# A convolution kernel's first loads: a smaller uncast head as one transfer, and the first pair's cast load moved behind the identity

## The chip, the core and the metric

The kernel runs on one core of one Trainium2 chip. The time is the device time of one execution in microseconds (us); smaller is better. Where a run was profiled, the "span" is the time from its first to its last instruction, about 1.8 us less than the measured time. All "landings" are the moments at which the trace shows the completion of a transfer on the last of the 16 DMA engines, if nothing else is said.

## The reference, cut to what matters

A 3 x 3 convolution with padding 1, in float32, of 16 images of 64 channels and 64 x 64 points, to 128 output channels:

```python
x      = randn(16, 64, 64, 64)                       # float32, 16.8 MB
weight = randn(128, 64, 3, 3) * (random(...) > 0.9)  # float32, 0.29 MB
output[b, co] += weight[co, ci, kh, kw] * x_pad[b, ci, kh:kh+64, kw:kw+64]
# output: (16, 128, 64, 64) float32, 33.6 MB
```

Every input byte has to be read and every output byte written: 50.6 MB.

## The kernel before

Two images make a "pair": 2 x 64 channels fill the 128 partitions. TensorE computes with bf16. Loads that convert float32 to bf16 on the way ("cast loads") are issued by GpSimd. Since the first products should not wait for them, the first 36 rows of pair 0, the "head", are loaded as float32 by the sync engine's queue, in two pieces, and cast by VectorE and ScalarE:

```python
HEAD = 36
nc.sync.dma_start(out=w_sb, in_=weight...)
x_head = const_pool.tile([128, HEAD, W], FP32, name="x_head")
for a, b in ((0, 9), (9, HEAD)):
    nc.sync.dma_start(out=x_head[:, a:b, :], in_=pair(0)[:, a:b, :])
nc.gpsimd.dma_start(out=xs[0][:, HEAD:H, :], in_=pair(0)[:, HEAD:H, :])
ident = const_pool.tile([128, 128], BF16, name="ident")
make_identity(nc, ident)                  # two short GpSimd instructions
for p in range(1, NP):
    nc.gpsimd.dma_start(out=xs[p], in_=pair(p))
# ... (27 idle matmuls to warm TensorE, casts and transposes of the weights)
cast_x(nc.vector.tensor_copy, 0, 9)
# ...
cast_x(nc.scalar.copy, 9, 18)
# ...
cast_x(nc.vector.tensor_copy, 18, HEAD)
```

Pair 0 begins with two "direct" products of 8 rows each (rows 0 to 15; they read rows 0 to 16). All other rows go in blocks of 16, for which GpSimd first adds neighbouring rows:

```python
def twos(p, o, r0):
    s = s_pool.tile([128, 8, W], BF16, name="s")
    nc.gpsimd.tensor_tensor(out=s, in0=xs[p][:, r0:r0+16:2, :],
                            in1=xs[p][:, r0+1:r0+16:2, :], op=ADD)
    # ... TensorE: 6 matmuls on s, 24 on xs[p]; VectorE adds and writes to o
for p in range(NP):
    # ... blocks of the pair, then
    if not last:
        for n in range(2):
            nc.sync.dma_start(out=out[2*p+n], in_=o[n])      # 2 MB each
    # the last pair in four pieces of 1 MB
```

## Time and profile before

| | before |
|---|---|
| time, median of the first 4 runs | 132.19 us (131.78 to 132.26) |
| span of the profiled run | 130.3 us |
| TensorE goes on with the second direct product at | 14.71 us |
| TensorE begins the first matmul on GpSimd's sums at | 18.50 us |
| end of the chain's TensorE part | 117.10 us |
| last store landed | 129.16 us |
| DMA queue empty (holes) | about 92 to 94.7 and 104 to 107.5 us |

### The profile page before, as it was taken

The page shows a single profiled execution, that of the slowest core. Times are in us where ns is not written, and L with a number is a line of the kernel's source. Part 1 is how long each engine was busy: PE and PEld are TensorE (multiplying, and loading weights), DVE is VectorE, ACT ScalarE, POOL GpSimd, SP SyncE. Part 2 cuts the span into 40 slices and gives each one's busy share as a digit, 9 for nine tenths or more (in the row PEclk, how much of TensorE's full clock was granted, in tenths as well). Part 3 has the DMA queues.
Part 4 walks back from the last instruction along what each step waited for, and adds up shares of the span by engine and source line. Part 5 has one row for each costly group of instructions (what it writes and reads, how often), then busy time and mean ns, then how long its engine had stood idle before and what let it go on. Part 6 is the DMA issues. An engine that isn't in the chain of part 4 may idle for free.

```text
span 130.3 us, 2488 instructions
## 1 busy us (share of the span) xinstructions
PE 110.6 (85%) x1002; PEld 56.0 (43%) x1002; DVE 83.0 (64%) x136; ACT 38.0 (29%) x70; POOL 40.7 (31%) x45
## 2 busy tenths in 40 slices
PE   6662499999999999999999999999999999993000
PEld 6430144445444544454445445544544454440000
DVE  0350425778777868787777777777777777777000
ACT  3500313333333333333243333333333333330000
POOL 6900463333333333333333333324333330000000
PEclk9985559999999999999999999999999999999655
DMA  4999999999999999999999999999599929999990
GB/s 136 217 297 228 216 209 226 209 216 216 302 325 307 327 322 314 362 428 438 423 425 428 433 423 433 428 428 443 244 408 403 403 86 402 458 385 415 415 410 18
DMA packets 4188, 42.99 MB, mean 330 GB/s; under 512 B 464, under 2 KB 464, under 8 KB 976
## 3 DMA queue, kind: packets, MB, share of 16 engines
q1 hardware_dynamic: 3024, 35.03, 64.6%
q0 software_dynamic: 1152, 7.80, 29.1%
q8 instruction: 8, 0.13, 0.4%
q14 instruction: 4, 0.03, 0.1%
HBM read 17.07 MB, written 33.55 MB: 389 GB/s over the span
## 4 chain that ended last, share of the span: by engine, by line
PE 79%; DMA 9%; DVE 1%; issue 1%; SPq 1%; ACT 1%; DVEq 0%
PE ps L136 79%; DMA x_head<-in_x_dram 9%; DVE o L169 1%; ACT x L88 1%; DVEq L215 0%; SPq L63 0%; SPq L60 0%; DVEq L169 0%
## 5 line engine op out<-in xcount | busy, mean ns | idle before, releaser
L136 PE MATMUL ps<-x,wT 64*128 64x504 bf16 (+3 forms) x780 | 91.4, 381 | 6.7 <-ACT x L88 4.2
L169 DVE TENSOR_TENSOR o<-ps,pc 128x512 f32<-128x512 f32 x124 | 77.8, 686 | 22.4 <-PE ps L136 20.1
L136 PEld LDWEIGHTS <-wT 64*128 64x128 bf16 x966 | 52.4, 96 | 60.4 <-issue 10.4
L155 POOL TENSOR_TENSOR s<-x 128x512 bf16<-128x512 bf16 x31 | 35.6, 1152 | 65.6 <-PE ps L136 43.4
L162 ACT COPY pc<-ps 128x512 f32<-128x512 f32 x62 | 33.3, 589 | 64.3 <-issue 61.8
L136 PE MATMUL ps<-s,wT 64*128 64x512 bf16 (+1 forms) x186 | 25.8, 380 | 0.0
L88 DVE CAST x<-x_head 128x576 bf16<-128x576 f32 (+1 forms) x2 | 1.2, 611 | 7.5 <-DMA x_head<-in_x_dram 7.5
L75 PE MATMUL ps<-idle_rhs 128*128 128x128 bf16 x27 | 3.1, 313 | 1.0 <-DVE idle_rhs L72 1.0
L68 POOL DMA_DIRECT2D x<-in_x_dram x7 | 3.7, 551 | 0.0
L150 DVE COPY o<-ps 128x512 f32<-128x512 f32 x2 | 1.4, 688 | 3.4 <-PE ps L136 3.4
L75 PEld LDWEIGHTS <-idle_rhs 128*128 128x128 bf16 x27 | 2.8, 149 | 1.0 <-DVE idle_rhs L72 1.0
L88 ACT CAST x<-x_head 128x576 bf16<-128x576 f32 x1 | 0.7, 672 | 8.2 <-DMA x_head<-in_x_dram 8.2
L92 DVE CAST w_bf<-w_sb 128x192 bf16<-128x192 f32 (+1 forms) x4 | 1.2, 360 | 2.5 <-DMA w_sb<-in_weight_dram 2.5
L149 ACT COPY o<-ps 128x512 f32<-128x512 f32 x2 | 1.2, 582 | 3.6 <-PE ps L136 3.6
L92 ACT ACT_TABLE_LOAD x1 | 1.3, 1283 | 0.7 <-PEq L204 0.7
L98 PE MATMUL ps<-ident,w_bf 128*128 128x128 bf16 x9 | 1.2, 308 | 0.0
L92 ACT CAST w_bf<-w_sb 128x64 bf16<-128x64 f32 (+1 forms) x2 | 0.7, 417 | 1.4 <-DMA w_sb<-in_weight_dram 1.4
L102 DVE TENSOR_TENSOR wT<-ps,wT 128x384 bf16<-128x384 f32 x2 | 1.0, 549 | 0.0
L98 PEld LDWEIGHTS <-w_bf 128*128 128x128 bf16 x9 | 0.8, 130 | 0.4 <-DVE w_bf L92 0.4
L64 POOL DMA_DIRECT2D x<-in_x_dram x1 | 0.7, 696 | 0.8 <-POOLq L204 0.8
L72 DVE MEMSET idle_rhs<- 128x64 uint32 x1 | 0.1, 112 | 0.8 <-PEq L204 0.8
L111 ACT CAST wT<-ps 128x384 bf16<-128x384 f32 x1 | 0.5, 478 | 0.4 <-PE ps L98 0.4
(8 smaller groups left out, 1.9 us busy)
## 6 DMA issues: line engine op xcount, KB each, us to landing
out_dram<-o SPq DMA_DIRECT2D x14, 2048.0 KB, 14.4
x<-in_x_dram POOLq DMA_DIRECT2D x7, 1024.0 KB, 26.1
out_dram<-o SPq DMA_DIRECT2D x4, 1024.0 KB, 9.4
x_head<-in_x_dram SPq DMA_DIRECT2D x1, 864.0 KB, 12.3
x<-in_x_dram POOLq DMA_DIRECT2D x1, 448.0 KB, 8.8
w_sb<-in_weight_dram SPq DMA_DIRECT2D x1, 288.0 KB, 2.7
x_head<-in_x_dram SPq DMA_DIRECT2D x1, 288.0 KB, 6.0
```

Of the source, the lines that this page charges most:

```text
L68: nc.gpsimd.dma_start(out=xs[p], in_=pair(p))
L75: nc.tensor.matmul(idle_ps, idle_rhs, idle_rhs, start=True, stop=True)
L88: copy(out=xs[0][:, a:b, :], in_=x_head[:, a:b, :])
L92: copy(out=w_bf4[:, g, a:b, :], in_=w_v[:, k : k + b - a, :])
L98: nc.tensor.matmul(wps[:, j, :], src, ident, start=True, stop=True)
L102: nc.vector.tensor_tensor(out=wT[:, g], in0=wps, in1=wT[:, G1], op=SUB)
L136: nc.tensor.matmul(ps[n][:, lo:hi, c_lo:c_hi], tap(g, kw, n), src[q, a:b:step, c_lo + kw - 1 : c_hi + kw - 1], start=(i == 0), stop=(i == ...
L149: nc.scalar.copy(out=o[0][:, r0 : r0 + rows, :], in_=ps[0])
L150: nc.vector.tensor_copy(out=o[1][:, r0 : r0 + rows, :], in_=ps[1])
L155: nc.gpsimd.tensor_tensor(out=s, in0=xs[p][:, r0 : r0 + 16 : 2, :], in1=xs[p][:, r0 + 1 : r0 + 16 : 2, :], op=ADD)
L162: nc.scalar.copy(out=c, in_=shared[n])
L169: nc.vector.tensor_tensor(out=o[n][:, first : r0 + 16 : 2, :], in0=ps[n], in1=pc[n], op=ADD)
```

## The change

The intent, in its author's words: "Only 18 rows of the first pair loaded uncast, as one transfer behind the weights; GpSimd issues the cast loads of all other rows straight away". The two direct products read 17 of these 18 rows.

```diff
-    HEAD = 36
+    HEAD = 18
...
-    for a, b in ((0, 9), (9, HEAD)):
-        nc.sync.dma_start(out=x_head[:, a:b, :], in_=pair(0)[:, a:b, :])
-    nc.gpsimd.dma_start(out=xs[0][:, HEAD:H, :], in_=pair(0)[:, HEAD:H, :])
+    nc.sync.dma_start(out=x_head, in_=pair(0)[:, 0:HEAD, :])
     ident = const_pool.tile([128, 128], BF16, name="ident")
     make_identity(nc, ident)
+    nc.gpsimd.dma_start(out=xs[0][:, HEAD:H, :], in_=pair(0)[:, HEAD:H, :])
...
-    cast_x(nc.scalar.copy, 9, 18)
+    cast_x(nc.scalar.copy, 9, HEAD)
     difference(G01, ps0)
     difference(G21, ps2)
-    cast_x(nc.vector.tensor_copy, 18, HEAD)
```

So there are three edits in one: fewer uncast rows (A), one transfer in place of two (B), and pair 0's cast load behind the identity in GpSimd's order (C). C makes GpSimd issue that load a little later, not sooner: at 1.43 us in place of 1.23 in the two traces.

## The prediction

> **What bounds the kernel now.** I read the page's digit rows first (slices of 3.26 us: PE is at 9 from the sixth slice on, DMA from the second), then the chain that ended last in order of time, then the timeline of the first 30 us, the DMA issues, and last the stages. The chain's middle:
>
> ```profile
> 1.65 12.31 DMA x_head<-in_x_dram
> 13.96 0.02 issue
> 13.98 0.68 ACT x L88
> 14.66 0.04 issue
> 14.71 102.39 PE ps L136 x936
> ```
>
> Columns: start, length, what. One transfer, the second piece of the uncast head (rows 9 to 35), holds the chain for 12.31 us; then TensorE runs without a gap until 117.10. So TensorE's start is what can be won, as long as nothing else bounds the end. Timeline (start, length, engine, line, what, count, idle before it and who ended it):
>
> ```profile
> 1.23 0.70 POOL L64 DMA_DIRECT2D x<-in_x_dram  x1 [0.79 <-POOLq L204]
> 7.21 0.46 DVE L88 CAST x<-x_head 128x576 bf16<-128x576 f32 x1 [2.58 <-DMA x_head<-in_x_dram]
> 7.72 2.77 PE L136 MATMUL ps<-x,wT 64*128 64x512 bf16 x18 [2.48 <-DVE x L88]
> 14.71 4.02 PE L136 MATMUL ps<-x,wT 64*128 64x512 bf16 x18 [4.22 <-ACT x L88]
> 18.50 1.14 PE L136 MATMUL ps<-s,wT 64*128 64x512 bf16 x6
> ```
>
> The first 8 output rows run at 7.72 on the first piece, then TensorE idles 4.22 us, and the next 18 matmuls take 4.02 us, where an unthrottled product of 24 takes 2.77 us in the same timeline. Stages (window, length, busy time of PE, PEld, DVE, ACT, POOL, granted clock, DMA share, GB/s):
>
> ```profile
> 7.72:10.49 2.77, 2.77 (x18) 1.17 (x18) 1.34 (x3) 0.00 (x0) 0.00 (x0) 0.71 1.10 281
> 14.71:18.50 3.79, 3.79 (x18) 1.48 (x19) 0.63 (x2) 0.43 (x1) 3.36 (x3) 0.50 1.04 218
> ...
> 52.00:92.00 40.00, 40.00 (x378) 20.03 (x376) 30.97 (x50) 13.76 (x26) 14.88 (x13) 1.00 1.01 422
> 92.00:94.70 2.70, 2.70 (x30) 1.42 (x28) 2.12 (x5) 1.07 (x2) 1.16 (x1) 1.00 0.49 200
> 94.70:104.00 9.30, 9.30 (x90) 4.59 (x86) 7.47 (x12) 3.12 (x6) 3.17 (x3) 1.00 1.00 421
> 104.00:107.50 3.50, 3.50 (x38) 1.82 (x34) 2.57 (x5) 1.18 (x3) 1.44 (x2) 1.00 0.21 84
> ```
>
> The clock is 0.50 just when TensorE restarts. And the DMA engines are full (share 1.0, 420 GB/s) everywhere except in two holes, at 92 and at 104 us, where the queue is empty because the next pair's stores are not yet issued (in the trace, pair 5's at 93.46, pair 6's at 106.27). So there are two bounds close together: TensorE's chain, and a DMA queue with only those two holes.
>
> Issues (bytes each, us to landing):
>
> ```profile
> x_head<-in_x_dram SPq DMA_DIRECT2D x1, 864.0 KB, 12.3
> x<-in_x_dram POOLq DMA_DIRECT2D x1, 448.0 KB, 8.8
> x_head<-in_x_dram SPq DMA_DIRECT2D x1, 288.0 KB, 6.0
> ```
>
> The sizes are those written: the cast transfer writes 448 KB but reads 896 KB.
>
> **What the Trainium skill says.** "DMA: Bandwidth & Descriptors", section "Queues, rings and completion order": each DMA engine goes round its queues packet by packet. The trace agrees: its packet records show a 6,912-byte head packet (0.275 us) alternating with GpSimd's cast packets, 0.285 us (28 rows), and later 0.625 us (64 rows of pair 1). Fourteen engines have reported the piece by 10.5 us, but two stragglers, by then alternating with pair 1, send their last packet at 12.7 and report at 13.8 and 13.96, and the semaphore waits for the slowest. Same page, "Issuing engines are not separate DMA queues": all issuers share the same 16 engines; the full stages above move 420 GB/s, with or without two queues at work. So the change can reorder bytes but not speed them. "TensorE: Matmul & The Clock Gate", Part 1: the clock is halved after a mostly idle window of about 3.4 us and restored after a busy one, the windows running freely. The trace's clock record agrees: half clock from 8.90 to 19.14 us, 10.24 = 3 x 3.41; windows start at 5.48, 8.90, 12.31, 15.72.
>
> **The change, part by part.**
> 1. *Bytes.* Weights and pair 0 are 0.295 + 2.097 = 2.39 MB read either way. Before, 36 rows uncast (1.18 MB) and 28 cast; after, 18 uncast (0.59 MB) and 46 cast (1.51 MB). At 420 GB/s this takes 5.7 us in both.
> 2. *Head.* Per engine: 8 weight packets of 0.093 us, as now (1.75 to 2.6 us), then 8 packets of 4,608 bytes at 2 x 0.093 = 0.185 us, 1.5 us. The first cast packet now starts at 3.54, 2.3 us after its issue at 1.23. After the change GpSimd first builds the identity (0.23 + 0.29 us and gaps), issues at about 1.9, and its first packet comes at about 4.2: the head has the engines alone 0.7 us longer. But packets stall for about 1 us between 3.2 and 5 us now (durations up to 1.13 us in place of 0.093), and the first 9-row piece was in at 7.2, not at 3.9. An engine that still owes five packets at 4.2 alternates with cast packets of 0.46 us (46 rows): 5 x 0.64 = 3.2 us, plus 0.6 us of completion. I put the head at 7.7 us, 0.5 us later than the 9-row piece now. DVE's cast of rows 0 to 8 (0.46 us) and ACT's of rows 9 to 17 (0.67 us) then run side by side, so both direct blocks of 8 rows run without a break from about 8.2. The old 18-row DVE cast (0.76 us) disappears, beside other work.
> 3. *Cast rows 18 to 63.* 8 packets of 0.46 us per engine, 3.7 us, from 4.2, with the rest of the head between them: about 9.3, landed at 10.0 (the present piece lands at 10.0 too). No straggler can alternate with pair 1, since pair 1 stands behind it in the same ring. GpSimd's first sum then takes 1.15 us: ready at 11.2.
> 4. *TensorE.* 36 matmuls, two side by side: 0.108 us each at full clock (30 in 3.24 us, from 22.06 to 25.30), 0.21 at half (18 in 3.79 us). From 8.2 to 8.9 warm (6 matmuls), half clock through the window 8.9 to 12.3 (16), then warm for the other 14 (1.5 us): done at 13.8. The sum is ready by then. Now the same point is 18.50, of which another 0.3 us is saved since 18.50 to 19.14 runs at half clock. **TensorE gains 18.5 + 0.3 - 13.8 = 5.0 us.**
> 5. *Which DMA allows how much of it.* Pair 4's last store lands at 94.94 on the slowest engine. From there, six 2 MB stores' worth is left (pairs 5, 6, 7). In the saturated stretch one takes 4.86 us (landings at 57.87, 62.73, 67.59, ...), 5.0 on the slowest engine (54.97 to 94.94 for eight): 30.0 us, plus some 1 us for two instruction fetches (0.93 us each in the trace): 94.9 + 31 = 125.9, against 129.16 now. So **the queue allows only about 3.3 us**, whatever TensorE does; the loads still start at 1.75 and lose their early 1 us as now. Buffers do not interfere: the tightest reuse of an output tile has over 9 us to spare.
>
> Sum: the smaller of 5.0 and 3.3 counts: 132.2 - 3.3 = **128.9 us**.
>
> **Rivals.**
> (a) *The DMA queue closes its holes and becomes the bound* (my central case). For: two holes of 2.7 x 0.51 + 3.5 x 0.79 = 4.1 us only, and the last 8.4 MB follow the last hole without a break. Against: the fastest engines have 5.9 us (pair 6's first landing 112.36 against 91.89 + 3 x 4.86 = 106.47); if the slow ones catch up, all 5.0 come through: 127.2.
> (b) *The head arrives late.* Nine rows had to land first, now eighteen, against larger cast packets. An engine owing all 8 packets at 4.2 would need 8 x 0.64 = 5.2 us: head at 10, matmuls from 10.5, half clock until 15.7 (24 matmuls), done at 17.0: gain 1.8, 130.4. For: one engine's last piece of the first head now came at 6.57, 1.5 us after all others. Against: even so the 4.2 us gap is gone.
> (c) *The cast rows are late*, as GpSimd issues them 0.7 us later and they are 1.64 times the bytes. They would have to land after 12.6 to matter; 10.0 is expected. Worth under 1 us.
> (d) *Warm clock throughout*, if the head lands near 6.5: directs done at about 11, TensorE gains 7; the queue then takes all beyond its limit, so still 128 to 129.
>
> **Range and chances.** TensorE's gain is 1.8 to 7, the queue's limit 2.3 to 5, and the smaller counts; 2% is 2.6 us. I give a late head 1 in 8 and a queue limit under 2.6 us 1 in 5: 0.875 x 0.8 = 0.7 for faster by over 2%, and the rest within 2%. Slower needs a mechanism that I do not see. Range 127.5 to 130.3.
>
> **What would show it.** Head landing at 7 to 8.5 and no idle of TensorE between the two direct blocks; the chain no longer naming the second head piece; TensorE's first matmul on the sums at about 13.8; clock at half only to 12.3; TensorE's end at about 112; and, decisive, no holes in the DMA row at 92 and 104 us and a longer tail after TensorE's end (12.0 us now, 13 to 14 then). If holes remain and the end still moved by 5, part 5 was too strict; if matmuls begin after 10 us, part 2 was wrong.

## The result, and the profile after

The changed kernel takes 127.76 us (median of 4 runs, 127.17 to 128.07) against 132.19 us. A ratio here is the mean time of one kernel's fast runs over that of the other's of the same rounds, so it is not quite the ratio of the medians: 0.9666, with a 95% interval of 0.9623 to 0.9708. It is faster, by 4.4 us or 3.3%.

The chain of the changed kernel, in order of time (start, length, what), at the place that answers to the one shown of before:

```profile
1.18 5.17 DMA x_head<-in_x_dram
6.34 0.02 issue
6.37 0.47 DVE x L87
6.84 0.04 issue
6.88 103.44 PE ps L134 x954
110.32 0.01 DVEq L167
```

The head is in at 6.34, and TensorE runs from 6.88 to 110.32 without a wait that the chain would name. It ends 117.10 - 110.32 = 6.8 us sooner than before. The timeline says the same of the restart:

```profile
1.43 0.70 POOL L65 DMA_DIRECT2D x<-in_x_dram  x1
6.88 5.33 PE L134 MATMUL ps<-x,wT 64*128 64x512 bf16 x36 [1.43 <-DVE x L87]
9.99 3.37 POOL L153 TENSOR_TENSOR s<-x 128x512 bf16<-128x512 bf16 x3 [4.17 <-DMA x<-in_x_dram]
12.03 0.82 PE L134 MATMUL ps<-s,wT 64*128 64x512 bf16 x6
```

The 4.22 us gap between the direct products is gone, and the first matmul on the sums comes at 12.03 in place of 18.50. GpSimd's first sum is ready at about 11.15 (9.99 plus 1.15), so it holds nobody up in this trace.

But the span is only 130.3 - 126.3 = 4.0 us shorter. The stages of the changed kernel (window, length, busy time of PE, PEld, DVE, ACT, POOL with counts, granted clock, DMA share, GB/s), in the same windows as before:

```profile
52.00:92.00 40.00, 40.00 (x378) 20.68 (x376) 31.04 (x50) 13.30 (x25) 14.42 (x13) 1.00 1.01 405
92.00:94.70 2.70, 2.70 (x28) 1.33 (x25) 1.97 (x4) 1.07 (x2) 1.15 (x1) 1.00 0.98 419
94.70:104.00 9.30, 9.30 (x90) 4.85 (x88) 7.26 (x13) 3.22 (x6) 2.31 (x2) 1.00 0.99 421
104.00:107.50 3.50, 3.50 (x36) 1.76 (x32) 2.77 (x5) 1.07 (x2) 0.00 (x0) 1.00 1.04 445
```

The holes at 92 (share 0.49 before) and 104 us (0.21 before) are closed: 0.98 and 1.04. The last store lands at 125.15 where it was 129.16. From the end of the chain's TensorE part to the end of the span it was 130.3 - 117.1 = 13.2 us, and now it is 126.3 - 110.3 = 16.0 us. Of TensorE's 6.8 us, 2.8 are given back as waiting in the queue.

The issues of the changed kernel (KB written, us to landing) answer to the three loads shown of before:

```profile
x<-in_x_dram POOLq DMA_DIRECT2D x1, 736.0 KB, 8.4
x_head<-in_x_dram SPq DMA_DIRECT2D x1, 576.0 KB, 5.2
```

### The profile page after: what moved, and what is told of

It reads as the page before. It is cut to its first block, busy times and chain, and to the rows that moved or that the text cites.

```text
span 126.3 us, 2486 instructions
## 1 busy us (share of the span) xinstructions
PE 108.9 (86%) x1002; PEld 57.2 (45%) x1002; DVE 82.3 (65%) x135; ACT 38.1 (30%) x70; POOL 40.8 (32%) x45
## 3 DMA queue, kind: packets, MB, share of 16 engines
HBM read 17.07 MB, written 33.55 MB: 401 GB/s over the span
## 4 chain that ended last, share of the span: by engine, by line
PE 82%; DMA 4%; DVE 1%; issue 1%; DVEq 0%; SPq 0%
PE ps L134 82%; DMA x_head<-in_x_dram 4%; DVE o L167 1%; DVEq L213 0%; DVE x L87 0%; SPq L60 0%; DVEq L167 0%
## 5 line engine op out<-in xcount | busy, mean ns | idle before, releaser
L134 PE MATMUL ps<-x,wT 64*128 64x504 bf16 (+3 forms) x780 | 90.0, 378 | 1.4 <-DVE x L87 1.4
L134 PEld LDWEIGHTS <-wT 64*128 64x128 bf16 x966 | 53.7, 95 | 52.2 <-issue 3.0
L87 DVE CAST x<-x_head 128x576 bf16<-128x576 f32 x1 | 0.5, 459 | 1.5 <-DMA x_head<-in_x_dram 1.5
## 6 DMA issues: line engine op xcount, KB each, us to landing
out_dram<-o SPq DMA_DIRECT2D x4, 1024.0 KB, 12.1
```

Of the source, the lines that this page charges most:

```text
L87: copy(out=xs[0][:, a:b, :], in_=x_head[:, a:b, :])
L134: nc.tensor.matmul(ps[n][:, lo:hi, c_lo:c_hi], tap(g, kw, n), src[q, a:b:step, c_lo + kw - 1 : c_hi + kw - 1], start=(i == 0), stop=(i == ...
```

## The experiments

The theory to be tested: (1) in the kernel before TensorE's chain sets the end, in the changed kernel the DMA queue does, with some 2.5 us of TensorE's gain unused; (2) the second head piece was late because its packets had to take turns with pair 1's. The rivals: TensorE sets the end in both; the queue does in both; the head was late by itself; only one of the edits A, B and C matters.

**On runs.** Each call of several kernels shared a chip and its own runs of the kernel before: 27, 27, 28 and 11 runs, with medians of 131.47, 131.35, 131.29 and 131.50 us. They spread much more than the first four: from 127.43 to 133.81 us. Eleven of these 93 runs lie under 129.5 us and the rest at 129.96 or above. A run counts as slow when it is over 1.5% above the fastest of its kernel, so in these rounds most of the ordinary runs of before are called slow, and ratios over the "fast" ones compare with the lucky ninth part. The profiled run of before (132.03 us) is an ordinary one. There is only one core here and no second die in play. I therefore give medians of all runs, beside the ranges, and use no ratio from these rounds to tell how large an effect is. The ratio of the result above takes all its eight runs, since no quick run of before was among the four. With the medians of e1's call the gain is 3.85 us (131.47 to 127.62) and not 4.4. Nearly all runs of the changed kernel and its variants count as fast, so these can be compared with each other. What the quick runs of before are is taken up below.

### Does TensorE set the end, or the queue?

**The yardstick, e1_after_again**: the changed kernel, unedited.

> The changed kernel itself, as the yardstick of this chip and these rounds. Every theory: 127.2 to 128.1 us, 3.2 to 3.6% under the kernel before. Because the throttle's windows run freely, TensorE's first matmuls on the sums should move between runs, while the end stays, if the DMA queue sets the end.

Measured: 127.62 us (6 runs, 127.51 to 128.06). The head is in at 6.04, the first matmul on the sums comes at 11.82 (12.03 in the first trace), and the last store lands at 124.56.

**e2_before_pad11, e3_after_pad11, e4_after_pad22**: useless matmuls, 0.216 us each at full clock, behind pair 0's direct products.

```diff
                     direct(p, o, r, rows)
+                pad = [psum_pool.tile([128, 8, W], FP32, name="ps") for _ in range(2)]
+                for i in range(11):        # 22 in e4
+                    nc.tensor.matmul(pad[i % 2], ident, xs[0][:, 0:8, :], start=True, stop=True)
```

> The kernel before with 11 full matmuls (11 x 0.216 = 2.4 us) of no use between pair 0's direct blocks and the rest. Theory (TensorE's chain sets the end of the kernel before, the DMA queue has holes): the whole 2.3 to 2.4 us comes out at the end, 134.5 us, and the hole at 104 us grows by as much. Rival (the DMA queue sets the end already): under 0.5 us, 132.5.

> The same 2.4 us of useless matmuls in the changed kernel. Theory (TensorE now ends some 2.5 us before the queue needs it): nearly nothing at the end, 0 to 0.5 us over the changed kernel, although TensorE ends 2.4 us later. Rival (TensorE's chain sets the end in the changed kernel too): 2.4 us, so 130.1.

> 22 such matmuls, 4.75 us, in the changed kernel. Theory: the slack of about 2.5 us is used up and the rest shows, 2.0 to 2.5 us over the changed kernel, near 130. Rival (TensorE sets the end): 4.75 us over, 132.5. Rival (TensorE does not matter at all): no difference.

| kernel | added to TensorE | median, all runs | against its own base |
|---|---|---|---|
| before + 11 | 2.48 us in the trace | 133.92 us (6 runs, 133.67 to 134.74) | +2.45 (131.47) |
| changed + 11 | 2.48 us | 127.96 us (6 runs, 127.49 to 128.06) | +0.34 (127.62) |
| changed + 22 | 4.85 us | 129.92 us (22 runs, 128.43 to 131.80) | +2.3 (127.62) |

In the kernel before, the whole delay comes out at the end; in the changed one nearly nothing of the same delay does, and of twice the delay about half. That is the picture of a slack of some 2.5 us, and both rivals (TensorE in both, the queue in both) fall. The chain of e3, for the place of the delay (the second line is the padding):

```profile
6.43 3.99 PE ps L134 x36
10.42 2.48 PE ps L183 x11
12.90 98.23 PE ps L134 x918
```

One caution: in this traced run the 36 direct matmuls took 3.99 us, where the profiled run of the changed kernel needed 5.33 us, as the throttle happened to be open. So the trace alone shows TensorE's end at 111.13, only 1.0 us later than the yardstick's; the verdict rests on the medians. The runs of e4 fall into two groups, 128.4 to 128.9 and 129.9 and above. Why, I did not settle: the mean clocks of the two groups overlap.

**e9_before_less_load, e10_after_less_load**: the opposite test. The queue gets 2.1 MB less to do. Their outputs are wrong, which doesn't matter for the times.

```diff
-    for p in range(1, NP):
+    xs[NP - 1] = xs[NP - 2]
+    for p in range(1, NP - 1):
         nc.gpsimd.dma_start(out=xs[p], in_=pair(p))
```

> Wrong result on purpose: the kernel before without the load of pair 7 (pair 7 is worked out from pair 6's rows), 2.1 MB or 4.87 us less for the queue. Theory (TensorE's chain sets the end): no change, within 0.3 us of the kernel before in these rounds, only larger holes. Rival (the queue sets it): up to 4.9 us less.

> Wrong result on purpose: the changed kernel without the load of pair 7. Theory (the queue sets the end and TensorE has 2 to 2.5 us to spare): 2 to 2.5 us less than the changed kernel's 127.6, so 125.1 to 125.6, and then a hole in the queue before pair 6's stores as in the kernel before. Rival (TensorE sets the end): no change, 127.6. Rival (the queue alone, with TensorE far ahead): the whole 4.9 us, 122.7.

Measured: the kernel before with less load 131.55 us (6 runs, 128.03 to 132.15) beside 131.29 of before: no change. The changed kernel with less load 125.01 us (6 runs, 124.58 to 125.66), 2.6 us less than the yardstick, which ran in another call (e11, of the same call, is at 128.03). Taking work from the queue helps only the changed kernel, and by the size of the slack, not by the 4.87 us that the load costs. In e10's stages the hole ahead of pair 6's stores is back, so there TensorE sets the end again:

```profile
94.70:100.00 5.30, 5.30 (x54) 2.85 (x52) 4.37 (x8) 1.92 (x4) 1.90 (x2) 1.00 0.55 229
100.00:103.00 3.00, 3.00 (x32) 1.58 (x30) 2.53 (x4) 0.91 (x3) 0.41 (x1) 1.00 1.04 437
```

TensorE's part of the chain ends at 110.06 in that trace, as in the yardstick (110.10): the 2.6 us are the queue's alone.

One more count from the traces fits: the time from the end of TensorE's part of the chain to the landing of the last store. It is 12.0 to 12.1 us in the kernel before, e2, e4, e9 and e10, but 13.9 in e3, 14.5 in the yardstick and 14.8 in the changed kernel. I read what exceeds 12.1 as TensorE's lead over the queue.

### Which part of the change does it?

**e5_head18_only**: edits A and B without C.

```diff
+    nc.gpsimd.dma_start(out=xs[0][:, HEAD:H, :], in_=pair(0)[:, HEAD:H, :])
     ident = ...
     make_identity(nc, ident)
-    nc.gpsimd.dma_start(out=xs[0][:, HEAD:H, :], in_=pair(0)[:, HEAD:H, :])
```

> The changed kernel, but GpSimd issues the cast load of pair 0 ahead of the identity, as before. Theory (the 18-row head does it, the order on GpSimd is a detail): head in within 1 us of the changed kernel's (6.0 to 6.3 us), and since the changed kernel has some 2 us to spare at the queue, the time within 0.5 us of it, 127.5 to 128. Rival (the head needs the 0.5 us of quiet that the new order gives): head at 8 us or later, time 129 or more.

Measured: 127.35 us (6 runs, 127.23 to 127.61), the head in at 6.00. The order is not needed when the head is 18 rows in one transfer. It is even 0.27 us under the yardstick, but that was timed in another call, and I do not call it faster.

**e6_order_only**: edit C alone; 36 rows in two pieces, as before.

```diff
-    nc.gpsimd.dma_start(out=xs[0][:, HEAD:H, :], in_=pair(0)[:, HEAD:H, :])
     ident = ...
     make_identity(nc, ident)
+    nc.gpsimd.dma_start(out=xs[0][:, HEAD:H, :], in_=pair(0)[:, HEAD:H, :])
```

> The kernel before (36 rows uncast in two pieces), only with the identity ahead of pair 0's cast load. Theory (the second piece is held up by pair 1's packets, not by pair 0's order): second piece still at 13 to 14 us, 131.5 to 132.2 us, as before. Rival (the order gives the gain): second piece at 10 to 11 us and some 128 to 129 us.

Measured: 127.69 us (6 runs: 127.33, 127.43, 127.55, 127.82, 129.66, 129.85). My theory missed, and the rival held: moving one line behind two instructions of GpSimd, 0.5 us of work, is enough by itself, in four runs of six. It moves the issue by only 0.19 us (1.23 to 1.42), as those two instructions now run in time that GpSimd had spent waiting. In the traced run, one of the four, the second head piece lands at 9.55 in place of 13.96, and the first cast packet goes out at 4.61. Its chain:

```profile
1.65 7.90 DMA x_head<-in_x_dram
...
10.30 100.22 PE ps L136 x936
```

The bytes are the same as before, and the queues too. What differs is seen in the DMA queues between 9.6 and 13 us (packets, MB, share). First the kernel before:

```profile
q0 software_dynamic: 86, 0.70, 97.7%
q1 hardware_dynamic: 13, 0.06, 4.2%
```

And with the order alone changed, the only queue at work in that window:

```profile
q0 software_dynamic: 91, 0.75, 104.7%
```

In the kernel before, 8 of the head's 128 second-piece packets are sent after 9.6 us (the 13 counts some 4-byte completion packets too). Each has to wait for one of pair 1's packets of 0.625 us, or for more than one, and the whole head waits for them. With the order changed none is left by then.

Counted in the packet records: of those 128 packets, 51 went out after pair 1's first packet in the kernel before. In the two other traces of kernels that load as it does (e2 and e9), 81 and 74 did. With the order alone changed it was 3, and in the changed kernel none. So the question is which queue runs dry first on an engine: the head's, or pair 0's cast load. If the cast load is done first, pair 1's packets are next in its ring, and the rest of the head takes turns with them.

**e12_one_piece36**: this explanation makes a prediction of its own. If turns are what counts, packets matter and not bytes. The same 36 rows as one transfer are 8 packets per engine, in place of 16. So edit B alone:

```diff
-    for a, b in ((0, 9), (9, HEAD)):
-        nc.sync.dma_start(out=x_head[:, a:b, :], in_=pair(0)[:, a:b, :])
+    nc.sync.dma_start(out=x_head, in_=pair(0)[:, 0:HEAD, :])
```

> The kernel before, order on GpSimd and 36 uncast rows unchanged, but the head as one transfer (8 packets of 9,216 bytes per engine) in place of two (16 packets). Theory formed after the run of the order alone (an engine takes a packet from each ring in turn, so what counts is which ring's packets run out first: sixteen head packets lose to eight cast packets and then meet pair 1's big ones, eight do not): the head is in at 8.5 to 9.5 us, no head packet is sent after 9.6 us, TensorE ends near 111 to 114 and the time is 127.5 to 129.5. Rival (36 uncast rows are too many bytes beside the casts): head at 13 us or later, 131 to 132.

Measured: 127.73 us (6 runs, 127.44 to 128.06), beside 131.50 of before (11 runs). The head of 36 rows is in at 7.76, sooner than the 8.5 to 9.5 expected, no packet of it goes out after pair 1's first, and the rival falls. All 36 rows come 6.2 us sooner than before by being one transfer.

```profile
1.18 6.58 DMA x_head<-in_x_dram
...
8.29 103.69 PE ps L135 x954
```

One thing keeps this from being a proof about turns alone. With the head as one transfer, pair 0's first cast packet also comes later, at 5.32 here and at 4.74 in e5, although it is issued at 1.24 in both, as before (first packet at 3.54 to 4.08). A later start of the cast packets helps the head just as in e6. Both belong to the same race, fewer turns to take and a rival that starts later, and for 36 rows no run has the one without the other. For 18 rows e7 below has: twice the packets, cast packets that start no sooner, and a later head. Why the cast packets start later behind larger head packets is open.

**e8_before_hold**: the kernel before, but GpSimd issues pairs 1 to 7 only once the head is in, by casting the head's last row itself.

```diff
+    nc.gpsimd.tensor_copy(out=xs[0][:, HEAD-1:HEAD, :], in_=x_head[:, HEAD-1:HEAD, :])
     for p in range(1, NP):
         nc.gpsimd.dma_start(out=xs[p], in_=pair(p))
...
-    cast_x(nc.vector.tensor_copy, 18, HEAD)
+    cast_x(nc.vector.tensor_copy, 18, HEAD - 1)
```

> The kernel before, but GpSimd issues the loads of pairs 1 to 7 only after the whole head has landed (it casts the head's last row itself and so waits for it). Theory (alternating with pair 1's 16 KB reads is what made the second piece late): second piece at about 10 to 10.5 us instead of 13.9, and TensorE goes on about 3.5 us sooner; but the queue is empty from about 10.5 to 13, pair 1 lands near 18 and the queue works 2 to 3 us later, so the end is 130 to 131.5. Rival (the second piece is late by itself): second piece at 13 to 14 us still, and the end at 132 or more.

Measured: the second piece is in at 10.61 in place of 13.5 to 14, which is what the theory said: without pair 1's packets there are no stragglers. The time was a miss: 133.08 us (6 runs, 131.15 to 133.91), not 130 to 131.5. The cause is in the chain. GpSimd now issues its seven loads, one after another, before its first sum:

```profile
11.95 3.18 POOL x L69 x6
15.13 1.18 POOL s L156
...
16.36 99.96 PE ps L137 x918
```

TensorE's first matmul on the sums waits until 16.36. And the queue stands still meanwhile: a DMA share of 0.06 from 10.0 to 12.7 us in that trace, time that the end does not get back. The last store lands at 129.97.

**e7_two_pieces**: the changed kernel with its 18 rows in two pieces (A and C without B).

```diff
-    nc.sync.dma_start(out=x_head, in_=pair(0)[:, 0:HEAD, :])
+    for a, b in ((0, 9), (9, HEAD)):
+        nc.sync.dma_start(out=x_head[:, a:b, :], in_=pair(0)[:, a:b, :])
```

> The changed kernel with its 18 rows as two transfers (9 and 9) on the same queue. Theory (one or two transfers is a detail, the bytes count): rows 0 to 8 at about 5, rows 9 to 17 at about 6.5, TensorE starts about 1 us sooner, the end unchanged at 127.5 to 128 as the queue sets it. Rival (a second transfer is what strands the head): rows 9 to 17 at 9 us or later, a gap of TensorE of over 2 us, and 129 or more.

Measured: 128.47 us (22 runs, 127.64 to 129.65). The pieces land at 4.71 and 7.94 in the traced run:

```profile
5.41 2.69 PE L135 MATMUL ps<-x,wT 64*128 64x512 bf16 x18
8.69 2.12 PE L135 MATMUL ps<-x,wT 64*128 64x512 bf16 x18 [0.59 <-ACT x L88]
11.93 0.82 PE L135 MATMUL ps<-s,wT 64*128 64x512 bf16 x6 [1.12 <-POOL s L154]
```

TensorE starts at 5.41, 1.2 to 1.5 us sooner than in the two traces of the changed kernel, as expected, but rows 9 to 17 come later than the whole head does as one transfer (6.04 and 6.34), and TensorE waits 0.59 us for them and 1.12 us for GpSimd's sum, behind pair 0's cast load (landed at 10.58). Its first matmul on the sums is at 11.93, between those of the changed kernel's two traces. The rival, with its gap of over 2 us, falls, but the time is 0.5 us above the range I expected and 0.85 us above the yardstick. The traced run was one of the quicker ones (127.80), so where the slower ones lose is open.

This is also the comparison that e12 lacks. In six traces that load as the changed kernel does (its two, e3, e4, e10 and e11) the first cast packet goes out at 4.23 to 4.58 and the head is in at 5.89 to 6.43. In e7 the first cast packet goes out no sooner, at 4.68, and 43 head packets of 2,304 bytes are then still to come, half the bytes of the changed kernel's 42 packets of 4,608; still the head is complete at 7.94. So splitting the head makes it later without an earlier start of the cast packets, and without more bytes. Its last packets go out one by one, the last at 7.09, beside cast packets of up to 1.8 us. That they wait for their turns fits, but with one trace of e7 it is argued.

**e11_late_issue**: the changed kernel, with pairs 3 to 7 issued only after GpSimd's three sums of pair 0. The question was the slow packets between 3 and 5 us.

```diff
-    for p in range(1, NP):
+    for p in (1, 2):
         nc.gpsimd.dma_start(out=xs[p], in_=pair(p))
...
+        if p == 0:
+            for q in range(3, NP):
+                nc.gpsimd.dma_start(out=xs[q], in_=pair(q))
```

> The changed kernel, with GpSimd issuing only pairs 1 and 2 early and pairs 3 to 7 after its three sums of pair 0. Theory A (the slow packets at 3 to 5 us come from GpSimd issuing transfers meanwhile): packets of the head and of pair 0 run at their plain 0.185 and 0.455 us, pair 0 is in about 1 us sooner, and as the queue sets the end, it is 0.5 to 1 us sooner too, 126.7 to 127.1. Theory B (they come from the first cast packets themselves, or from the memory): no change, 127.6.

Measured: 128.03 us (22 runs, 127.40 to 129.06); the head is in at 6.43, pair 0's cast rows at 10.29. Single packets of 1.26 us (head) and 2.16 us (cast) are still there. Theory A falls; what the slow packets come from stays open, as theory B names two causes that no run here tells apart.

### What the quick runs of before are

About one run in nine of the kernel before takes 127.4 to 129.5 us, as long as a run with the head in time. That fits the race between two queues, which a small difference in the start of the cast packets decides: the first of them went out at 3.54, 3.99 and 4.08 us in three traces of kernels that load as before. With the order alone changed, two runs of six were still at 129.7 and 129.9. But no quick run of before was profiled, so this is argued and not shown.

## Why the prediction was right

The time (128.9 predicted, 127.76 measured) lies in the range, and the prediction's mechanism is the one that the runs show: TensorE wins more than the queue lets through. Several steps on the way were off, and two numbers came out right by luck (points 2 and 3).

1. **Bytes.** Right: 17.07 MB are read from HBM on both pages.
2. **Head.** Predicted at 7.7, measured at 6.34 and 6.04 in two traces and 6.00 in e5's. (My own terms, 4.2 + 3.2 + 0.6, add up to 8.0 and not to 7.7.) The first cast packet came at 4.28, near the 4.2 worked out, but by luck: I had added the identity's time to GpSimd's issue and put it at 1.9. In fact the identity ran in the 0.79 us that GpSimd had waited before, the issue was at 1.43, and the first packet came 2.85 us after it, not 2.3. The mis-sized term was how much of the head an engine still owes then: I put it at five packets of eight and their turns at 3.2 us. In the trace, 42 of all 128 head packets were sent after that moment, 2.6 per engine on average, and the last at 5.84, which leaves room for two or three such turns.
3. **Cast rows.** 10.0 predicted, 9.85 measured (10.21 in the yardstick). The number is right, the sum is not: from 4.2, eight packets of 0.46 and five of 0.185 end at 8.8, where I wrote 9.3.
4. **TensorE's gain.** Predicted 5.0, measured 6.5 at the first matmul on the sums (18.50 to 12.03) and 6.8 at the end of its part. Two terms were off. The start was 1.3 us sooner (point 2). And I had let the throttle's windows begin where they did in the trace of before; in the changed kernel's trace the half clock ends at 9.65, not at 12.31, so that it took 5.15 us (6.88 to 12.03) and not 5.6 to the first matmul on the sums. The windows run freely, as I had quoted from the Trainium skill ("TensorE: Matmul & The Clock Gate", Part 1), so their edges could not be carried over.
5. **The queue's limit.** Predicted 3.3, measured 4.0 in the landings (129.16 to 125.15) and in the spans. From 94.91, when pair 4's last store lands on the slowest engine, the rest took 30.2 us, where I had 31: 30.0 for six stores and 1 for two instruction fetches of 0.93 each, that is for about one of them on this engine. Two fetches of 0.94 and 0.93 us are in this trace too (at 97.48 and 111.01). The kept records do not name the engine, so whether they ran on another engine or the stores took less is not shown. This term makes most of the error of the total. The rest of the way to the median, 4.4, is within the runs' spread. One reading was loose, that the full stages move 420 GB/s with or without two queues at work: the lines with 420 GB/s hold little but stores. Where cast loads share the engines of the kernel before the view shows less (383 GB/s from 52 to 57 us, 427 from 57 to 92), at the same DMA share of 1.01, since it counts a cast load by the bytes that it writes.
6. **What would show it.** The holes did close, and TensorE has no idle time between the direct blocks. The head (6.34, not 7 to 8.5), the first matmul on the sums (12.03, not 13.8) and the end of the half clock (9.65, not 12.3) all came sooner than named. The tail after the last matmul is 14.8 us (111.5 to 126.3; I had said 13 to 14). TensorE's end is 110.3 instead of about 112.

The prediction did not say which of the three edits does it, and the expectation of e6 shows that I would have said wrongly. I had read that the stragglers alternate with pair 1, but did not ask what lets pair 1 in. That pair 1 "stands behind it in the same ring" I said of the cast rows, and it holds before the change too. What the runs show is that it is enough if the head's packets run out before pair 0's cast packets do. Fewer rows in one transfer (e5), one transfer of all 36 rows (e12), or a later cast load (e6, in four runs of six) each get the whole gain. Fewer rows alone, in two pieces and in the old order, was not run. And since the queue caps it at about 4 us, having all three adds nothing that the runs can show. Of the rivals, (a) held, with its cap at 4.0; (b) and (c) did not come to pass. But the 12.6 of (c) was too late a limit. In the traces of e10 and e11 the clock was at full speed during the direct products, as in (d), and these took 3.99 us. The cast rows landed at 10.43 and 10.29 there, and TensorE waited 1.13 and 0.69 us for GpSimd's sum. So with a warm clock GpSimd's first sum holds TensorE up next, which (d), with its gain of 7, left out. No version clearly beat the changed kernel; e5 equals it.

## What to carry to other kernels

When transfers on two queues compete, count packets and turns, and not bytes alone: in this case the early transfer did better as few large packets (e12, and the changed kernel against e7), and it had to run out before the other queue's next large transfer began. And before crediting a change with what it takes off the critical chain, look for the holes in the DMA row: their size is the most that an earlier start can bring, and what exceeds it only waits. Delaying the suspected engine on purpose, and relieving the other one on purpose, tells in two short kernels which of them sets the end.

## What the Trainium skill lacked or had wrong

- "DMA: Bandwidth & Descriptors", "Queues, rings and completion order", has the turns at packet granularity, and the trace agrees that there are turns. It lacks the consequence that unequal packets make unequal shares, and that splitting a transfer can make it later: rows 9 to 35 landed at 13.96 us as the second of two pieces, and all 36 rows at 7.76 as one; 18 rows at 7.94 in two pieces, and at 6.04 and 6.34 as one. And while the page's typical packet holds 9 to 17 descriptors, the turns here went by single rows of a partition: one series of the kernel before's last head packets goes out at 9.99, 10.87, 11.75 and 12.62, 0.88 us apart, which is about one packet of 0.275 and one of 0.625.
- The same page, "Specifications", gives about 1 us to the first byte of a GpSimd-issued load. That is near what e8 shows with the queue idle: 1.3 us from the start of pair 1's issue to its first packet (11.40 to 12.66). The page lacks how it grows beside other transfers: 2.3 us in the kernel before (1.23 to 3.54), and 4.1 with the one-piece head of 36 rows in front (1.24 to 5.32).
- "TensorE: Matmul & The Clock Gate", Part 1, warns that clock records can be unreliable. It does not say that nothing is known before a profile's first record: the changed kernel's profile shows clock 1.00 from the start, its first record is at 9.65 us, and until 8.11 us the weight loads of successive pairs of matmuls start 0.43 us apart (7.26, 7.69, 8.11), twice the full-clock time of 0.216 us.
- The same page as in the first two points says that two of the 16 engines are usually slower, and guesses at a cause on GpSimd's path. No page has a figure for how far apart the engines end a run of plain stores: in the changed kernel the last store lands at 121.47 us on the first engine and at 125.15 on the last, which are 3.7 us of the end. Which engine is last, the kept records do not say, and the cause was not looked for.
